# Four PSUM banks for the first eighth of the MLP's first product, and weight tiles of their own for the gates

## The chip, the cores and the metric

The kernel runs on one core of a Trainium2 chip. The metric is the time of one execution on the device in microseconds. Shown is the median of several runs; beside it stands one execution taken by the hardware profiler, from which all rows of this document come. Engines are named as in the profile: PE is the matmul engine (PEld its weight loads), DVE the vector engine, ACT the scalar engine, POOL the general one, SP the queue that issues the DMAs.

## What is computed

A decoder trunk of two layers over 256 tokens with 2048 channels in float32. The first layer mixes with a gated linear recurrence (RG-LRU), the second with dilated attention; a squared-ReLU MLP follows each.

```python
for i in range(DEPTH):                       # DEPTH = 2
    h = _rmsnorm(x, mix_norm[i])
    if i % N_MIXERS == 0:
        x = x + _rglru_block(h, ...)         # w_in, conv, gates w_a and w_x, scan, w_out
    else:
        x = x + _dilated_attention_block(h, ...)
    x = x + _mlp(_rmsnorm(x, mlp_norm[i]), mlp_w1[i], mlp_w2[i])
return _rmsnorm(x, final_norm)

def _mlp(h, w1, w2):
    u = jnp.square(jax.nn.relu(jnp.einsum('bsd,df->bsf', h, w1)))
    return jnp.einsum('bsf,fd->bsd', u, w2)  # 2048 -> 8192 -> 2048
```

In the recurrent block, the 2560 channels form ten heads of 256. Each head has two gates, two products with 256 x 256 matrices, that are fed by the head's convolved channels.

## The kernel before

**Units.** All weights come in units of 128 partitions x 2048 floats (1 MB). A unit is loaded into a `raw` tile (three of them, L82), and split into a high half `whi` (ACT, L102) and a low half `wlo` (DVE, L106). Each product is then the sum of three matmuls: high by high, high by low, low by high (`stand_w` L245 with the weights standing still and 256 tokens moving; `stand_x` L254 with the activations standing still). `whi` and `wlo` are rings of three tiles each: the split of a unit waits until the matmuls of the unit three back are done. The weights of the gates of one head are a unit too, but of half the width (1024 columns, `gate` L446), and take a whole place in the rings.

**Order.** Every engine's instructions stand in an order written out by hand. Items (L134) run one after another. Ahead of an item `before_unit` (L124) emits loads up to five units ahead, high halves up to two ahead and low halves up to two ahead; behind it `behind_unit` (L130) emits the next high half. What follows an item some items later (`after`, L161) is emitted behind it: the evacuation of its sums, the convolution, the gates' arithmetic. An engine that waits holds up all that is emitted behind. SP only issues loads; a load waits until the `raw` tile's low half was made.

**Recurrent block** (`plan_rec`, L431). From head 2 on a head's items are: P0 (first half of its recurrent channels), the gate of the head before, P1, P2 and P3 (second half, and the two halves of the multiplying branch). `xb_done` (L334) takes P0 and P1 into the convolution, `conv_split` (L354) splits the result for the gate, `gb_done` (L359) and `gelu_arg` (L366) take P2 and P3. `gate_run` (L373), `gate_sig`, `gate_exp`, `gate_mult`, `scan` and `y_split` (L387 to L429) follow the gate, one item apart. POOL does two products of a head, in `gate_exp` (L407, L408). The output projection follows in four chunks of 512 channels; `close_chunk` (L283) adds a chunk to the residual `xc` (`add_x`, L281), and the transposed chunk `xT` is the MLP's input. The factor of the norm, `rstdB`, is made last (`rstd_cols` L223, `rstd_rows` L235) and is not in `xT`: it is multiplied in when the sums of the first product are read (L486).

**PSUM.** Eight banks: four named `acc`, two `g`, two `tr`. Output projections, attention's products and most projections sum in `acc`; the gates and the MLP's first product in `g`; transposes in `tr`.

**MLP** (`plan_mlp`, L524). The first product's 8192 columns are done in eighths of eight units of 128 columns (j = 0 to 7), and the second product of an eighth runs between the units of the next. The first eighth has nothing to run between and so stands alone. `plan_start` (L534) runs its first two units, j = 0 and 4, in two pieces each, since the last chunk of `xT` comes late: 12 of 16 rows of j = 0, 12 of j = 4, then the last 4 of each. Then j = 1, 5, 2, 6, 3, 7 follow (L612). `u_done` (L481) reads the sums of a unit out of PSUM: DVE multiplies and clips (L486), ACT squares and makes the high half (L487, L489), DVE the low half a unit later (L495).

**Scopes.** Activations of a stage lie in a pool `lru` that is closed and opened again for each stage (L791 to L802), at the same place of the memory.

Of the kernel before, what the change touches and what calls it, by code (L numbers as in the profile page):

```python
# [10 lines left out]
F32 = mybir.dt.float32  # L11
F32R = mybir.dt.float32r
# [16 lines left out]
UW = 2048  # L29
# [12 lines left out]
HI_BUFS = 3  # L42
# [10 lines left out]
def trunk(ctx: ExitStack, tc: tile.TileContext, a: dict, out: bass.AP):  # L53
    nc = tc.nc
    P = 128

    perm = ctx.enter_context(tc.tile_pool(name="perm", bufs=1))
    wts = ctx.enter_context(tc.tile_pool(name="wts", bufs=1))
    psum = ctx.enter_context(tc.tile_pool(name="psum", bufs=1, space=bass.MemoryType.PSUM))
# [3 lines left out]
    units = []  # L63

    def unit(ap, width=UW):
        units.append({"ap": ap, "width": width})
        return len(units) - 1
# [6 lines left out]
    raw, split = {}, {}  # L74
# [14 lines left out]
    def make(i):  # L89
        if "load" in units[i]:  # L90
            units[i]["make"]()
            raw[i] = [(slice(0, UW), units[i]["source"]())]

    def new_hi(i):
        split[i] = (wts.tile([P, UW], F32R, name="whi", bufs=HI_BUFS),)

    def new_lo(i):
        split[i] += (wts.tile([P, UW], F32R, name="wlo", bufs=3),)

    def hi_piece(i, n):  # L100
        s, r = raw[i][n]
# [6 lines left out]
    def cut_hi(i):  # L108
        new_hi(i)
        for n in range(len(raw[i])):  # L110
            hi_piece(i, n)

    def cut_lo(i):
        new_lo(i)
        for n in range(len(raw[i])):
            lo_piece(i, n)
        del raw[i]
# [18 lines left out]
    def item(u, fn):  # L136
        items.append((u, fn))
# [21 lines left out]
    lru = Scope()  # L159

    def after(n, fn, *args):  # L161
        later.setdefault(now[0] + n, []).append((fn, args))
# [82 lines left out]
    def stand_w(ps, u, ks, w_at, first, last):  # L245
        hi, lo = split[u]
        for j, k in enumerate(ks):
            x = xT(k)
            s = slice((w_at + j) * 128, (w_at + j + 1) * 128)
            mm(ps, hi[:, s], x[:, 0:256], first and j == 0, False)  # L250
            mm(ps, hi[:, s], x[:, 256:512], False, False)
            mm(ps, lo[:, s], x[:, 0:256], False, last and j == len(ks) - 1)
# [12 lines left out]
    def acc_tile():  # L265
        return psum.tile([P, 512], F32, name="acc", bufs=4)

    accs = {}
# [255 lines left out]
    def plan_mlp(w1, w2, done):  # L524
        def plan_first(p, j):
            u = unit(w1[8 * p + j])

            def run():
                accs["u", p, j] = psum.tile([P, 512], F32, name="g", bufs=2)
                stand_w(accs["u", p, j][:, :S], u, range(KD), 0, True, True)  # L530
                after(0, u_done, p, j, accs.pop(("u", p, j)))
            item(u, run)

        def plan_start():  # L534
            us = [unit(w1[j]) for j in (0, 4)]
            for at, ks in enumerate((range(0, 12), range(12, 16))):
                for u, j in zip(us, (0, 4)):
                    def run(u=u, j=j, ks=ks, at=at):
                        if at == 0:
                            accs["u", 0, j] = psum.tile([P, 512], F32, name="g", bufs=2)  # L540
                        stand_w(accs["u", 0, j][:, :S], u, ks, ks[0], at == 0, at == 1)
                        if at == 1:
                            after(1 if j == 0 else 0, u_done, 0, j, accs.pop(("u", 0, j)))
                    item(u, run)
# [69 lines left out]
        for p in range(8):  # L614
# [5 lines left out]
            g = plan_group(p, 0) if p in GROUPS else {}  # L620
# [201 lines left out]
    for n in range(NCH):  # L822
        xg[n] = new_xg(n)
        rs = [wts.tile([P, UW], F32, name="raw", bufs=RAW_BUFS) for _ in range(3)] if n == 0 else rs
        for h in range(2 if n == 0 else 1):
            w = 2 if n == 0 else 4
# [11 lines left out]
        for h in range(2 if n == 0 else 1):  # L838
            w = 2 if n == 0 else 4
            for k in range(h * w, (h + 1) * w):  # L840
                nc.scalar.activation(t[:, k, 0:256], xg[n][:, k, :], AF.Identity, scale=pcol("mix0", 4 * n + k))
            for k in range(h * w, (h + 1) * w):
                nc.vector.scalar_tensor_tensor(t[:, k, 256:512], xg[n][:, k, :], pcol("mix0", 4 * n + k),  # L843
                                               t[:, k, 0:256].bitcast(F32), op0=OP.mult, op1=OP.subtract)
            for i in range(3):
                if n == 0 and h == 0:
                    new_hi(i)
                    new_lo(i)
                for at, (s, _) in enumerate(raw[i]):
                    if s.stop == n * 512 + (h + 1) * w * 128:  # L850
                        hi_piece(i, at)
                        lo_piece(i, at)
                        if s.start == 0:
                            accs["first", i] = acc_tile()
                            first[i] += (accs["first", i],)
                        ks = range(s.start // 128, s.stop // 128)
                        stand_w(accs["first", i][:, :S], i, ks, ks[0], s.start == 0, n == NCH - 1)
# [54 lines left out]
    for at in range(len(items) - 1, -1, -1):  # L912
        u = items[at][0]
# [86 lines left out]
```

## Time and profile before

| | us |
|---|---|
| median of three runs | 2189.44 (2188.41 to 2190.64) |
| the profiled execution's own time | 2186.37 |
| its span, first to last instruction | 2184.6 |
| PE busy in it | 2150.0 |
| DVE busy in it | 1602.2 |
| ACT busy in it | 1166.2 |

A row of the timeline reads: start and duration in us, engine, line, operation, the tile written and the tiles read, the shape, the count of merged instructions, and in brackets the idle time of the engine just before, with what ended it. A row of stretches reads: the stretch, its length, then for PE, PEld, DVE, ACT and POOL the busy time with the number of instructions in brackets, then the granted clock of PE, the share of the DMA engines and GB/s. A row of waits reads: engine, tile and line, what it waited for, us in total, times, the longest.

### The profile page before, as it was taken

To read this page: it belongs to the slowest core of one execution; us is meant where nothing else is said; L and a number is where in the kernel's file an instruction comes from. 1 tells how busy PE (TensorE), PEld (TensorE's weight loads), DVE (VectorE), ACT (ScalarE), POOL (GpSimd) and SP (SyncE) were. 2 spreads that over 40 slices of the span, in tenths; PEclk is the share of its full clock that TensorE was granted. 3 is DMA by queue.
4 is the path that set the end of the run, shared out by engine and by line. 5 is a ranking of instruction groups with operands and counts; after the bars stand their busy time and mean duration, and the time that the engine had idled before them with its cause. 6 is when DMAs were issued, how large, how long until landed. Compare 5 with 4: busy or idle time off the path is not lost.

```text
span 2184.6 us, 32102 instructions
## 1 busy us (share of the span) xinstructions
PE 2150.0 (98%) x13602; PEld 1944.2 (89%) x13602; DVE 1602.2 (73%) x1748; ACT 1166.2 (53%) x1261; POOL 81.3 (4%) x42
## 2 busy tenths in 40 slices
PE   7999999999999999999999999999999999999997
PEld 7999988999999999999888888889999999999996
DVE  8888865688888888787655555556888878887875
ACT  5777755554554555445545544555545544544543
POOL 2222100000000000000000000000000000000002
PEclk9999999999999999999999999999999999999999
DMA  6655565455465455554554444454564554545543
GB/s 220 213 190 190 183 222 180 174 203 221 138 248 189 177 195 207 185 223 163 179 198 156 172 174 173 157 191 161 206 231 144 222 213 154 218 187 193 212 175 134
DMA packets 61712, 413.56 MB, mean 189 GB/s; under 512 B 6784, under 2 KB 7168, under 8 KB 13440
## 3 DMA queue, kind: packets, MB, share of 16 engines
q1 hardware_dynamic: 61568, 411.51, 51.8%
q8 instruction: 106, 1.74, 0.3%
q14 instruction: 38, 0.31, 0.0%
HBM read 409.39 MB, written 2.10 MB: 188 GB/s over the span
## 4 chain that ended last, share of the span: by engine, by line
PE 80%; DVE 12%; ACT 5%; issue 2%; POOL 0%; DMA 0%; SPq 0%; DVEq 0%; ACTq 0%
PE acc L165 47%; PE g L165 27%; DVE wlo L106 7%; PE tr L165 4%; ACT whi L102 3%; DVE q L564 1%; ACT sT L181 1%; DVE xT L843 0%; DVE c L349 0%; DVE sT L182 0%; PE tr L205 0%; DVE aT L495 0%; DVE sw L506 0%; PE tr L664 0%; PE g L672 0%
## 5 line engine op out<-in xcount | busy, mean ns | idle before, releaser
L102 ACT ACTIVATE whi<-raw 128x2048 fp32r<-128x2048 f32 (+3 forms) x358 | 657.1, 1838 | 570.5 <-PE acc L165 313.9
L106 DVE TENSOR_TENSOR wlo<-raw,whi 128x2048 fp32r<-128x2048 f32 (+3 forms) x358 | 792.0, 2216 | 212.4 <-ACT whi L102 212.4
L165 PE MATMUL g<-xT,whi 128*128 128x256 f32 x4128 | 732.9, 281 | 5.8 <-DVE uu L486 5.8
L165 PEld LDWEIGHTS g<-xT,whi 128*128 128x128 f32 x4128 | 638.0, 188 | 15.2 <-DVE uu L486 6.3
L165 PE MATMUL g<-xT,wlo 128*128 128x256 f32 x2064 | 580.4, 281 | 2.1 <-DVE wlo L106 2.1
L165 PE MATMUL acc<-whi,aT 128*128 128x512 f32 x1840 | 580.5, 390 | 0.0
L165 PEld LDWEIGHTS acc<-whi,aT 128*128 128x128 f32 x1840 | 345.4, 188 | 69.6
L165 PEld LDWEIGHTS g<-xT,wlo 128*128 128x128 f32 x2064 | 395.3, 192 | 4.6 <-DVE wlo L106 4.6
L165 PE MATMUL acc<-wlo,aT 128*128 128x512 f32 x920 | 358.3, 389 | 0.0
L165 PE MATMUL acc<-whi,xT 128*128 128x512 f32 x768 | 245.9, 396 | 0.0
L165 PE MATMUL acc<-xT,whi 128*128 128x256 f32 x1248 | 223.5, 283 | 6.3 <-ACT whi L102 5.8
L165 PEld LDWEIGHTS acc<-wlo,aT 128*128 128x128 f32 x920 | 172.8, 188 | 33.5
L102 ACT ACTIVATE whi<-q 128x2048 fp32r<-128x2048 f32 x56 | 107.2, 1914 | 177.0 <-DVE q L564 137.8
L165 PEld LDWEIGHTS acc<-xT,whi 128*128 128x128 f32 x1248 | 195.0, 194 | 6.9 <-ACT whi L102 6.1
L165 PE MATMUL acc<-xT,wlo 128*128 128x256 f32 x624 | 178.2, 286 | 9.3 <-DVE wlo L106 9.0
L165 PEld LDWEIGHTS acc<-whi,xT 128*128 128x128 f32 x768 | 144.3, 188 | 30.7
L165 PE MATMUL acc<-wlo,xT 128*128 128x512 f32 x384 | 150.4, 392 | 0.0
L106 DVE TENSOR_TENSOR wlo<-q,whi 128x2048 fp32r<-128x2048 f32 x56 | 128.2, 2289 | 19.0 <-ACT whi L102 19.0
L165 PEld LDWEIGHTS acc<-xT,wlo 128*128 128x128 f32 x624 | 121.0, 194 | 12.0 <-DVE wlo L106 12.0
L102 ACT ACTIVATE whi<-qT 128x2048 fp32r<-128x2048 f32 x28 | 53.7, 1916 | 132.7 <-DVE qT L564 132.7
L106 DVE TENSOR_TENSOR wlo<-qT,whi 128x2048 fp32r<-128x2048 f32 x28 | 64.2, 2293 | 47.8 <-ACT whi L102 47.8
L165 PEld LDWEIGHTS acc<-wlo,xT 128*128 128x128 f32 x384 | 72.2, 188 | 15.1
(172 smaller groups left out, 1917.3 us busy)
## 6 DMA issues: line engine op xcount, KB each, us to landing
raw<-in_w SPq DMA_DIRECT2D x214, 1024.0 KB, 4.8
raw<-in_w_qkv SPq DMA_DIRECT2D x48, 1024.0 KB, 4.8
q<-in_w SPq DMA_DIRECT2D x42, 1024.0 KB, 6.9
raw<-in_w_in SPq DMA_DIRECT2D x35, 1024.0 KB, 4.8
raw<-in_w_out SPq DMA_DIRECT2D x20, 1024.0 KB, 4.8
raw<-in_w_o SPq DMA_DIRECT2D x16, 1024.0 KB, 4.8
raw<-in_w_g SPq DMA_DIRECT2D x10, 512.0 KB, 3.5
raw<-in_w_in SPq DMA_DIRECT2D x11, 256.0 KB, 6.1
```

The costliest lines, as they stand in the source:

```text
L102: nc.scalar.activation(split[i][0][:, s], r, AF.Copy)
L106: nc.vector.tensor_sub(split[i][1][:, s], r, split[i][0][:, s].bitcast(F32))
L165: nc.tensor.matmul(o, l, r, start=start, stop=stop, skip_group_check=True)
L181: nc.scalar.activation(hi_out, src, AF.Copy)
L564: nc.vector.tensor_add(q[to], q[a], q[b])
```

## The change

First, the sums of the first eighth (p = 0) of each MLP's first product are put in `acc` banks, of which there are four, and not in `g`, of which there are two; the other seven eighths stay in `g`. Second, a unit that is narrower than 2048 columns, which only the gates' ten units are, is split into tiles `ghi` and `glo` of its own (two of each, 1024 columns, in the stage's pool) and not into the rings `whi` and `wlo`. No instruction is added, removed or moved in any engine's order.

```diff
+    def cut_tile(i, name, bufs):
+        width = units[i].get("width", UW)
+        if width < UW:
+            return lru.tile([P, width], F32R, name="g" + name, bufs=2)
+        return wts.tile([P, UW], F32R, name="w" + name, bufs=bufs)
+
     def new_hi(i):
-        split[i] = (wts.tile([P, UW], F32R, name="whi", bufs=HI_BUFS),)
+        split[i] = (cut_tile(i, "hi", HI_BUFS),)
 
     def new_lo(i):
-        split[i] += (wts.tile([P, UW], F32R, name="wlo", bufs=3),)
+        split[i] += (cut_tile(i, "lo", 3),)
...
             def run():
-                accs["u", p, j] = psum.tile([P, 512], F32, name="g", bufs=2)
+                accs["u", p, j] = acc_tile() if p == 0 else psum.tile([P, 512], F32, name="g", bufs=2)
                 stand_w(accs["u", p, j][:, :S], u, range(KD), 0, True, True)
...
                         if at == 0:
-                            accs["u", 0, j] = psum.tile([P, 512], F32, name="g", bufs=2)
+                            accs["u", 0, j] = acc_tile()
                         stand_w(accs["u", 0, j][:, :S], u, ks, ks[0], at == 0, at == 1)
```

`acc_tile` (L265) is `psum.tile([P, 512], F32, name="acc", bufs=4)`.

## The prediction

> **What bounds the kernel now.** I read the page's totals first, then what the matmul engine waited for, over the span and inside two stretches.
>
> ```profile
> span 2184.6 us, 32102 instructions
> PE 2150.0 (98%) x13602; PEld 1944.2 (89%) x13602; DVE 1602.2 (73%) x1748; ACT 1166.2 (53%) x1261; POOL 81.3 (4%) x42
> ```
>
> PE is busy for 2150.0 of 2184.6 us. No instruction is added or removed by the change, so the most that it can win is idle PE time and what follows from it.
>
> ```profile
> PE acc L165 <- DVE wlo L106: 9.0, 9, 3.1
> PE g L165 <- DVE uu L486: 5.8, 2, 2.9
> PE acc L165 <- ACT whi L102: 5.8, 2, 5.4
> PEld g L165 <- DVE uu L486: 6.3, 2, 3.2
> PE acc L165 <- DVE wlo L106: 1.8, 6, 0.3
> PE acc L165 <- DVE wlo L106: 2.4, 1, 2.4
> ```
>
> Columns: total us, times, longest. The first four rows are of the whole span, the fifth is of 100 to 260 us (the gates' loop), the sixth of 60 to 100 us. Two things can be won by this diff: the two waits on `uu` (one at the start of each MLP) and the six small ones in the gates' loop. The rest of the `acc` rows lies before 60 us, where no gate has run yet, and the wait of 2.4 us has another cause (below).
>
> **Part one: four banks for the first eighth.** At the start of the first MLP:
>
> ```profile
> 388.45 1.39 DVE L281 TENSOR_TENSOR xc<-xc,acc 128x512 f32<-128x512 f32 x2 [0.66 <-PE acc L165]
> 391.11 2.29 DVE L106 TENSOR_TENSOR wlo<-raw,whi 128x2048 fp32r<-128x2048 f32 x1 [1.27 <-ACT whi L102]
> 399.66 3.71 ACT L102 ACTIVATE whi<-raw 128x2048 fp32r<-128x2048 f32 x2 [1.30 <-PE g L165]
> 400.99 0.38 PE L238 MATMUL tr<-con,rs 128*128 128x128 f32 x2
> 401.61 2.29 DVE L106 TENSOR_TENSOR wlo<-raw,whi 128x2048 fp32r<-128x2048 f32 x1 [2.27 <-ACT whi L102]
> 403.28 0.36 ACT L241 ACTIVATE rstdB<-tr 128x256 f32<-128x256 f32 x1
> 403.81 0.75 DVE L486 SCALAR_TENSOR_TENSOR uu<-g,rstdB 128x256 f32<-128x256 f32 x2
> 404.29 0.50 PE L165 MATMUL g<-xT,whi 128*128 128x256 f32 x2 [2.91 <-DVE uu L486]
> 404.48 2.28 DVE L106 TENSOR_TENSOR wlo<-raw,whi 128x2048 fp32r<-128x2048 f32 x1
> 404.60:408.00 3.40, 3.40 (x32) 3.40 (x31) 2.83 (x3) 1.22 (x4) 0.00 (x0) 1.00 0.86 306
> ```
>
> Blocks j=0 and j=4 hold both `g` banks. They are emptied by L486, which needs `rstdB` (L241), which stands on ACT behind two weight splits. The third block, j=1, waits for a `g` bank until the first L486 ends. With `acc` it takes one of four banks. The blocks j=0 and j=4 take the banks of the output projection's third chunk and j=1 and j=5 those of its last; the last chunk's `acc` was read at 388.45 + 1.39 = 389.84. The fifth block, j=2, is the first that comes back to a bank of j=0. It starts two blocks later, and a block is 48 matmuls, 5.1 us at the 32 in 3.40 us of the last row (a stretch: PE's count stands in the first bracket, the granted clock third from the end), so the L486 at 403.81 is about 7 us early for it.
>
> What is late next? For j=1 the low half was done at 391.11 + 2.29 = 393.40. For j=5 it is done at 401.61 + 2.29 = 403.90, wanted at about 401.2 + 5.1 = 406.3; for j=2 at 406.76, wanted at 411.4. Later splits wait for the block that frees their tile and move with PE. So nothing catches the gain, and I price it by the weight loads' wait, 6.3 us for both MLPs (the matmul row, 5.8, counts only from the modelled end of the last transpose). The second MLP has the same picture:
>
> ```profile
> 1488.30 0.38 PE L238 MATMUL tr<-con,rs 128*128 128x128 f32 x2
> 1491.60 0.50 PE L165 MATMUL g<-xT,whi 128*128 128x256 f32 x2 [2.92 <-DVE uu L486]
> 1492.10:1495.50 3.40, 3.40 (x18) 3.40 (x18) 2.64 (x3) 1.06 (x3) 0.00 (x0) 0.52 0.93 316
> 85.80:89.20 3.40, 3.40 (x18) 3.40 (x18) 3.33 (x4) 3.38 (x6) 3.10 (x2) 0.52 0.95 317
> ```
>
> The last two rows are again stretches of 3.4 us behind a stall. Behind the one at 404 (row above) PE did 32 matmuls at clock 1.00; behind the one at 1491 it did 18 at 0.52, and as few behind the 2.4 us stall before 84.5. A stall can thus cost 14/32 of 3.4 us, 1.5 us, on top. In the profiled execution one of the two `uu` stalls paid it, so 1.5 us goes with them. Bounds: 0 (neither pays) and 3.0 (both). Part one: 6.3 + 1.5 = 7.8 us.
>
> The Trainium skill (TensorE: Matmul & The Clock Gate, Part 1) says that the clock is halved after at least one idle window of about 3.4 us, in windows that run freely. By that rule a stall of 3.2 us would be too short, nothing would be saved beyond the 6.3, and the time is that of the rival on the clock below. The row at 1492 disagrees, 0.52 after a shorter stall.
>
> **Part two: the gates' own weight tiles.** Gate units leave the ring of three `whi` and three `wlo`. One head of the steady loop (a projection P0, the gate, then P1, P2, P3):
>
> ```profile
> 122.16 1.92 ACT L102 ACTIVATE whi<-raw 128x2048 fp32r<-128x2048 f32 x1 [0.77 <-PE acc L165]
> 127.60 1.92 ACT L102 ACTIVATE whi<-raw 128x2048 fp32r<-128x2048 f32 x1 [3.52 <-PE acc L165]
> 130.56 1.90 ACT L102 ACTIVATE whi<-raw 128x2048 fp32r<-128x2048 f32 x1
> 121.42 0.69 DVE L182 TENSOR_TENSOR chl<-c,chl 128x512 fp32r<-128x512 f32 x1 [1.22 <-ACT chl L181]
> 125.59 0.69 DVE L423 TENSOR_TENSOR i<-i,gb 128x512 f32<-128x512 f32 x1
> 122.36 1.22 DVE L106 TENSOR_TENSOR wlo<-raw,whi 128x1024 fp32r<-128x1024 f32 x1
> 126.54 2.28 DVE L106 TENSOR_TENSOR wlo<-raw,whi 128x2048 fp32r<-128x2048 f32 x1
> 129.85 0.76 DVE L182 TENSOR_TENSOR aT<-i,aT 128x256 fp32r<-128x256 f32 x2 [1.04 <-ACT aT L181]
> 134.11 5.58 DVE L106 TENSOR_TENSOR wlo<-raw,whi 128x2048 fp32r<-128x2048 f32 x2
> 135.77 0.39 PE L165 MATMUL acc<-xT,whi 128*128 128x256 f32 x2
> 136.45 0.39 PE L165 MATMUL acc<-xT,wlo 128*128 128x256 f32 x1 [0.29 <-DVE wlo L106]
> 136.68 0.40 PE L165 MATMUL acc<-xT,whi 128*128 128x256 f32 x2
> 119.63 9.54 SPq L87 DMA_DIRECT2D raw<-in_w_in  x3
> raw<-in_w_in SPq DMA_DIRECT2D x35, 1024.0 KB, 4.8
> ```
>
> The split at 127.60 is the high half of P2. Its ring slot is that of the unit three back, P0, whose matmuls end at 127.5; so ACT stands 3.52 us, the aT split behind it is late, DVE stands 1.04 us at 129.85, and P2's low half (134.11, ends 136.40) is late for PE at 136.0. With the gate out of the ring the unit three back is the P3 of the head before, which had freed its slot at 122.16 (first row). The split then waits for its data: loaded from 119.63, 4.8 us later at 124.4, ended at 126.4. The aT split follows, since L423 is done at 125.59 + 0.69 = 126.28, and DVE goes on at 126.54 + 2.28 = 128.82, 1.03 us earlier. P2's low half ends at 135.4, 0.6 us early.
>
> What PE lost: from the row at 135.77 the next should start 0.23 later (two matmuls), it starts 0.68 later, and the pair behind 0.23 instead of 0.12 later: 0.57 us a head, six heads, 3.4 us. Is DVE the next bound?
>
> ```profile
> 127.51:152.68 25.17, 24.88 (x219) 24.68 (x217) 22.38 (x29) 19.09 (x23) 5.43 (x2) 1.00 0.55 190
> 135.42 2.13 POOL L407 TENSOR_TENSOR c<-c,i 128x512 f32<-128x512 f32 x1 [19.73 <-ACT i L394]
> 68.20 1.30 POOL L408 TENSOR_TENSOR gb<-gb,gw 128x512 f32<-128x512 f32 x1
> 63.29 0.63 ACT L181 ACTIVATE chl<-c 128x512 fp32r<-128x512 f32 x1 [4.76 <-POOL c L347]
> ```
>
> A head lasts 25.17 us. PE needs 25.17 - 0.57 = 24.60; DVE, without the 1.04, 24.13, with its other wait of 1.22 kept. So PE decides, by 0.47. The unknown is POOL. The two splits at 134.11 took 5.58 us, 1.0 more than twice 2.29, while POOL ran L407: they get in each other's way, and today the second split, which is early, pays. ACT's chain to L407 moves by about 2.1 us (the split at 130.56 can start when its data are there: the raw tile comes free with the gate's low half at 122.36 + 1.22 = 123.58, the load lands 4.8 us later at 128.4), so L407 comes near 133.3, and P2's low half starts near 133.1. If POOL comes first, it delays that split by at most its own 1.30, to about 136.7, later than today's 136.4. Bounds: 3.4 us won to 6 x 0.3 = 2 lost. I take 3.4, since DVE comes first and gains up to 0.47 more on PE with each head.
>
> The 2.4 us stall before 84.5 stays: ACT is without a pause from 63.29, where it waited for POOL's convolution, and no split of a tile waits there. The tiles' 16 KB per partition cost no instruction; the next scope lays its tiles over the same space, but opens only behind the output projection, when the last gate is long done. So 0.
>
> **Sum.** 7.8 + 3.4 = 11.2 us. The profiled execution took 2186.37, so 2175.2 for a like one; the median of the runs is 2189.44, 3.07 above it, and gives 2178.2.
>
> **Rivals.**
> - The gates' half gives nothing, because P2's low half now meets POOL or DVE's chain doesn't get ahead. For it: the 0.2 us between 133.1 and 133.3, and DVE's load. Against it: 0.6 us of room at P2. Time: 2189.44 - 7.8 = 2181.6.
> - The clock isn't part of it: whether a stall meets a half-clock stretch is chance (one of two did), and if the timed runs paid none, 6.3 + 3.4 gives 2179.7. By the rule of the Trainium skill told above, this is the case that holds.
> - Part one doesn't do what it says: j=1 finds another wait as long. For it: the wait's name is inferred. Against it: PE starts at 404.29, between the ends of the two L486 (a pair of 0.75 from 403.81), as it would if the first one held it, and its weights and the other bank are there by 394. Time: 2189.44 - 3.4 = 2186.0, not to be told from no change.
> - Slower: both POOL products (L407, L408) come ahead of P2's low half in every head. At 1.30 each it ends at 135.4 + 2.6 = 138.0, PE stalls 2.0 us for 0.45 now, and about half of such stalls also pay 1.5 us of clock, as before 85.8. Six heads: 6 x 1.55 + 3 x 1.5 = 13.8 us lost, less part one's 7.8: 2189.44 + 6.0 = 2195.4. It decides from the point where L408 starts before the split; against it, L408 waits for ACT L397, behind L407's own inputs. The Trainium skill (SBUF — State Buffer, on the shared port pair of VectorE and GpSimd) has this as an exclusive lock, first come first served; the 5.58 us agree with such a lock.
>
> **Chances.** Forecast 0.60 (own range 2175.5 to 2180.5), clock 0.10, gates nothing 0.18, part one nothing 0.07, slower 0.05. The range 2175.0 to 2184.0 holds the first three, the gates' case with part of its possible loss, and about 1 us of scatter (the runs spread from 2188.41 to 2190.64). About 0.2%, 4.4 us, is what a measurement of this kernel can tell from no change; the first three cases lie beyond it: faster 0.87, within 0.08, slower 0.05.
>
> **What would show it.** Right: no wait of PE on `uu`; the matmuls of j=1 directly behind the two transposes of L238, at 401.2 or a little earlier; clock 1.00 through the start of both MLPs; the 3.52 us of ACT before P2's split gone; no PE wait on `wlo` between 100 and 260 us; heads of 24.6 us; the 2.4 us stall still there. Wrong: a wait of PE on `acc` behind add_x or L486, heads of 25.2 us or more, or a POOL product ahead of P2's low half.

## The result

| | before, us | after, us | ratio, 95% interval |
|---|---|---|---|
| first comparison (4 and 4 runs) | 2188.93 (2187.90 to 2190.64) | 2173.74 (2173.12 to 2174.57) | 0.993 (0.9913 to 0.9947) |
| second comparison (21 and 5 runs) | 2186.27 (2180.39 to 2190.34) | 2175.25 (2173.29 to 2175.83) | 0.995 (0.9937 to 0.9963) |
| the profiled execution's own time | 2186.37 | 2173.91 | |

The change wins 15.2 us in the first comparison and 11.0 us in the second. The forecast was 11.2 us won and 2178.2 us, in a range of 2175.0 to 2184.0; the median of the first comparison lies 1.3 us below that range, that of the second 0.25 us inside it. The two waits that the prediction named went, at about their price. What was sized wrong is the clock that goes with one of them.

The page's totals of the changed kernel, and then what PE waited for (total us, times, longest). Lines of the code stand six further down than before: L165 is L171, L238 is L244, L486 is L492, L407 is L413.

```profile
span 2172.1 us, 32089 instructions
PE 2144.1 (99%) x13602; PEld 1940.1 (89%) x13602; DVE 1600.6 (74%) x1748; ACT 1167.5 (54%) x1261; POOL 78.9 (4%) x42
```

PE's waits, the first three rows over the span, the fourth between 60 and 100 us:

```profile
PE acc L171 <- DVE wlo L112: 8.1, 4, 2.7
PE acc L171 <- ACT whi L108: 6.1, 2, 5.9
PE g L171 <- DVE wlo L112: 2.2, 12, 0.2
PE acc L171 <- DVE wlo L112: 2.6, 1, 2.6
```

No wait on `uu` is left. Between 100 and 260 us PE waits for nothing any more. Between 60 and 100 us the stall of 2.4 us before the loop is still there, now 2.6 us.

The timeline at the start of the first MLP:

```profile
395.73 0.38 PE L244 MATMUL tr<-con,rs 128*128 128x128 f32 x2
395.87 0.48 PE L171 MATMUL acc<-xT,whi 128*128 128x256 f32 x2
394.40 3.72 ACT L108 ACTIVATE whi<-raw 128x2048 fp32r<-128x2048 f32 x2 [1.30 <-PE acc L171]
398.02 0.36 ACT L247 ACTIVATE rstdB<-tr 128x256 f32<-128x256 f32 x1
398.56 0.75 DVE L492 SCALAR_TENSOR_TENSOR uu<-acc,rstdB 128x256 f32<-128x256 f32 x2
```

And stretches of 3.4 us at the start of both (the count of matmuls in the first bracket, the granted clock third from the end):

```profile
395.87:399.27 3.40, 3.40 (x32) 3.40 (x31) 2.92 (x4) 2.78 (x4) 0.00 (x0) 1.00 0.00 0
1480.92:1484.32 3.40, 3.40 (x33) 3.40 (x31) 2.92 (x4) 2.78 (x4) 0.00 (x0) 1.00 0.00 0
```

The chain behind the transposes is unchanged: two splits on ACT, then `rstdB`, then L492. But j = 1 no longer stands behind it. It starts 0.14 us after the transposes instead of 3.30 us, and L492 reads j = 0 while j = 1 runs. The clock is 1.00 at both starts.

One head of the gates' loop (the gate starts at 125.99):

```profile
117.89 1.91 ACT L108 ACTIVATE whi<-raw 128x2048 fp32r<-128x2048 f32 x1
120.72 1.92 ACT L108 ACTIVATE whi<-raw 128x2048 fp32r<-128x2048 f32 x1 [0.92 <-PE acc L171]
126.07 1.92 ACT L108 ACTIVATE whi<-raw 128x2048 fp32r<-128x2048 f32 x1 [1.91 <-PE acc L171]
125.33 0.76 DVE L188 TENSOR_TENSOR aT<-i,aT 128x256 fp32r<-128x256 f32 x2
129.43 5.59 DVE L112 TENSOR_TENSOR wlo<-raw,whi 128x2048 fp32r<-128x2048 f32 x2
130.95 1.91 POOL L413 TENSOR_TENSOR c<-c,i 128x512 f32<-128x512 f32 x1 [18.59 <-ACT i L400]
132.82 3.35 POOL L414 TENSOR_TENSOR gb<-gb,gw 128x512 f32<-128x512 f32 x1
115.92 9.85 SPq L87 DMA_DIRECT2D raw<-in_w_in  x3
```

The same head as one stretch:

```profile
125.99:150.62 24.63, 24.63 (x218) 24.63 (x217) 22.21 (x29) 19.30 (x23) 5.22 (x2) 1.00 0.57 193
```

The high halves of P1, P2 and P3 are the first three rows. P2's starts 5.3 us ahead of the gate; before, it started 0.1 us behind it, after the wait of 3.52 us. The wait of 1.91 us that ACT now has is P3's, and nobody is late by it. DVE no longer waits at `aT`. P2's low half (the first of the two at 129.43) starts 3.4 us behind the gate instead of 6.6 us, 1.5 us ahead of POOL's L413. PE is busy through the whole head, 24.63 us.

**Where the 12.5 us between the two profiled spans are.** The same stages of both kernels: up to the second head's gate, seven heads of gates, up to the transposes of L238, the start of the first MLP, up to the second start, that start, the rest. Of before:

```profile
0.00:102.34 102.34, 88.60 (x678) 86.67 (x679) 83.64 (x128) 64.59 (x92) 28.84 (x21) 0.95 0.63 215
102.34:279.13 176.79, 174.95 (x1491) 172.61 (x1490) 155.90 (x197) 133.58 (x161) 38.04 (x14) 1.00 0.56 194
279.13:400.99 121.86, 121.80 (x609) 102.88 (x608) 66.44 (x56) 67.62 (x82) 3.23 (x2) 1.00 0.54 191
400.99:404.29 3.30, 0.39 (x5) 0.14 (x3) 2.69 (x3) 2.68 (x4) 0.00 (x0) 1.00 0.00 0
404.29:1488.30 1084.01, 1082.89 (x6397) 959.05 (x6397) 750.42 (x822) 553.46 (x604) 0.00 (x0) 1.00 0.51 187
1488.30:1491.60 3.30, 0.38 (x5) 0.14 (x3) 2.69 (x3) 2.67 (x4) 0.00 (x0) 1.00 0.00 0
1491.60:2184.60 693.00, 680.99 (x4428) 622.73 (x4428) 540.39 (x543) 341.57 (x318) 11.23 (x5) 0.99 0.51 190
```

And of after:

```profile
0.00:101.35 101.35, 86.51 (x679) 84.41 (x680) 84.40 (x129) 67.71 (x96) 28.87 (x21) 0.98 0.63 217
101.35:273.81 172.46, 172.46 (x1491) 171.50 (x1489) 155.97 (x200) 134.57 (x161) 35.86 (x14) 1.00 0.58 199
273.81:395.73 121.92, 121.86 (x609) 102.94 (x608) 64.38 (x54) 64.82 (x78) 2.87 (x2) 1.00 0.54 190
395.73:395.87 0.14, 0.14 (x4) 0.14 (x3) 0.00 (x0) 0.14 (x1) 0.00 (x0) 1.00 0.00 0
395.87:1480.78 1084.91, 1083.76 (x6399) 959.98 (x6398) 752.86 (x824) 556.04 (x607) 0.00 (x0) 1.00 0.51 186
1480.78:1480.92 0.14, 0.14 (x5) 0.14 (x3) 0.00 (x0) 0.14 (x1) 0.00 (x0) 1.00 0.00 0
1480.92:2172.10 691.18, 679.19 (x4431) 620.95 (x4428) 543.02 (x545) 344.12 (x321) 11.25 (x5) 1.00 0.51 191
```

| stage | difference, us | what it is |
|---|---|---|
| start-up | -0.99 | clock 0.95 against 0.98, untouched code |
| heads with gates | -4.33 | part two |
| up to the transposes | +0.06 | |
| first MLP's start | -3.16 | part one, the wait |
| first MLP and attention | +0.90 | the same work, a little slower |
| second MLP's start | -3.16 | part one, the wait |
| the rest | -1.82 | mostly the half-clock stretch behind the stall at 1491 |
| sum | -12.50 | |

So from profile to profile the forecast was 1.3 us off (2175.2 for 2173.91), and without the two stages in which the clock differs (-0.99 and -1.82) the change won 9.7 us, as 6.3 + 3.4 had it. That it agrees to the tenth is luck: the gates gave 0.9 us more than their 3.4, and 0.90 us was given back behind the first MLP's start. The medians differ by 2.7 us more than the profiles: before's profiled execution lies 2.6 us below its median, after's 0.2 us above. The experiments ask whether part one, part two or the clock is worth more in a usual run than in the profiled one.

### The profile page after: what moved, and what is told of

Read it like the earlier page. It is cut to its first block, busy times and chain, and to the rows that moved or that the text cites. A ratio compares the mean times of both kernels' runs of the same rounds, so it can differ in the third digit from the quotient of the medians.

```text
span 2172.1 us, 32089 instructions
## 1 busy us (share of the span) xinstructions
PE 2144.1 (99%) x13602; PEld 1940.1 (89%) x13602; DVE 1600.6 (74%) x1748; ACT 1167.5 (54%) x1261; POOL 78.9 (4%) x42
## 3 DMA queue, kind: packets, MB, share of 16 engines
q8 instruction: 106, 1.74, 0.3%
## 4 chain that ended last, share of the span: by engine, by line
PE 83%; DVE 10%; ACT 4%; issue 1%; POOL 0%; DMA 0%; SPq 0%; DVEq 0%; ACTq 0%
PE acc L171 53%; PE g L171 24%; DVE wlo L112 6%; PE tr L171 4%; ACT whi L108 2%; DVE q L570 1%; ACT sT L187 1%; DVE sT L188 0%; PE tr L211 0%; DVE aT L501 0%; DVE sw L512 0%; PE tr L670 0%; PE g L678 0%; DVE xT L849 0%; DVE sw L514 0%
## 5 line engine op out<-in xcount | busy, mean ns | idle before, releaser
L108 ACT ACTIVATE whi<-raw 128x2048 fp32r<-128x2048 f32 (+2 forms) x348 | 646.8, 1860 | 562.2 <-PE acc L171 336.5
L112 DVE TENSOR_TENSOR wlo<-raw,whi 128x2048 fp32r<-128x2048 f32 (+2 forms) x348 | 779.9, 2245 | 214.9 <-ACT whi L108 214.7
L171 PE MATMUL g<-xT,whi 128*128 128x256 f32 x3616 | 642.4, 281 | 0.0
L171 PE MATMUL acc<-whi,aT 128*128 128x512 f32 x1840 | 580.5, 390 | 0.0
L171 PEld LDWEIGHTS g<-xT,whi 128*128 128x128 f32 x3616 | 559.1, 188 | 8.7
L171 PE MATMUL g<-xT,wlo 128*128 128x256 f32 x1808 | 508.5, 281 | 2.2 <-DVE wlo L112 2.2
L171 PEld LDWEIGHTS acc<-whi,aT 128*128 128x128 f32 x1840 | 345.4, 188 | 69.6
L171 PE MATMUL acc<-wlo,aT 128*128 128x512 f32 x920 | 358.3, 389 | 0.0
L171 PEld LDWEIGHTS g<-xT,wlo 128*128 128x128 f32 x1808 | 346.2, 191 | 4.6 <-DVE wlo L112 4.6
L171 PE MATMUL acc<-xT,whi 128*128 128x256 f32 x1760 | 309.7, 281 | 6.5 <-ACT whi L108 6.1
L171 PEld LDWEIGHTS acc<-xT,whi 128*128 128x128 f32 x1760 | 270.7, 191 | 7.5 <-ACT whi L108 6.3
L171 PE MATMUL acc<-xT,wlo 128*128 128x256 f32 x880 | 247.2, 281 | 8.3 <-DVE wlo L112 8.1
L171 PE MATMUL acc<-whi,xT 128*128 128x512 f32 x768 | 245.9, 396 | 0.0
L171 PEld LDWEIGHTS acc<-wlo,aT 128*128 128x128 f32 x920 | 172.8, 188 | 33.4
L171 PEld LDWEIGHTS acc<-xT,wlo 128*128 128x128 f32 x880 | 168.0, 191 | 9.6 <-DVE wlo L112 9.4
L171 PEld LDWEIGHTS acc<-whi,xT 128*128 128x128 f32 x768 | 144.3, 188 | 30.6
L171 PE MATMUL acc<-wlo,xT 128*128 128x512 f32 x384 | 150.4, 392 | 0.0
L171 PEld LDWEIGHTS acc<-wlo,xT 128*128 128x128 f32 x384 | 72.2, 188 | 15.1
```

The source lines that it names most:

```text
L108: nc.scalar.activation(split[i][0][:, s], r, AF.Copy)
L112: nc.vector.tensor_sub(split[i][1][:, s], r, split[i][0][:, s].bitcast(F32))
L171: nc.tensor.matmul(o, l, r, start=start, stop=stop, skip_group_check=True)
```

## The experiments

The first four kernels of the table were timed beside the kernel before on one chip, the last four on another; two repeats at the end ran once each on a third. Times in the text are medians, those of the table means, and a difference is to the kernel before on the same chip (2188.91 on the first, 2186.27 on the second, 21 runs each). Each run also lists its mean granted clock to three places. From it I worked out what the run lost, (1 - clock) times its span, and what is left of its time then. One step in the last place is 2.2 us of a run, so only means over runs, and differences between kernels, say something. The column counts every half-clock stretch: also those of start-up, which five profiles show twice, one once and six not at all, and 2.8 to 4.5 us a run behind the last matmul, where they cost PE nothing.

| kernel, runs | mean us | lost to the clock | rest |
|---|---|---|---|
| before, first chip, 21 | 2188.9 | 10.5 | 2178.3 |
| banks alone, 5 | 2180.3 | 6.5 | 2173.8 |
| gates alone, 11 | 2183.0 | 10.5 | 2172.5 |
| before with the stalls filled, 11 | 2185.7 | 6.6 | 2179.1 |
| a third transpose, 5 | 2174.6 | 6.1 | 2168.5 |
| before, second chip, 21 | 2186.0 | 9.2 | 2176.8 |
| gates' high halves alone, 10 | 2181.7 | 9.4 | 2172.3 |
| gates' low halves alone, 10 | 2186.8 | 9.2 | 2177.6 |
| after with its stalls filled, 5 | 2171.9 | 2.2 | 2169.7 |
| after, 5 | 2174.9 | 7.0 | 2167.9 |

### Each part alone

The first kernel has only the two `acc_tile()` edits, the second only `cut_tile` and its two calls.

> The kernel before with the first half of the change alone: the first eighth of the first MLP product sums in the four acc banks, the gates' weights stay in the shared rings. Theory A (the prediction's terms): 6.3 us of wait and 1.5 us of clock go, 7.8 us below the kernel before, so about 2181.2. Theory B (the unprofiled runs of the kernel before lose more half-clock stretches behind the two stalls than the one that its profile shows): 10 to 12 us below, about 2178, and less scatter between runs. Theory C (the surplus of the change over its forecast lies in the gates' half): 7 to 8 us below here and 7 us or more in the run with the gates alone.

> The kernel before with the second half alone: the gates' units in tiles of their own, the first eighth still in the two g banks. Theory A: 3.4 us below the kernel before, about 2185.6, no wait of PE on wlo between 100 and 260 us, both waits of about 2.9 us on uu still there. Theory B: the same 3.4 to 4 us here. Theory C: 7 us or more below, about 2182.

The banks alone took 2181.01 us, 7.9 us won, ratio 0.9964 (0.9951 to 0.9976). The forecast for part one, 7.8 us, is met, but not by its terms. The wait is gone, 6.3 us. The table gives 4.0 us to the clock instead of 1.5, and the rest fell by only 4.5 us. In its profile the heads' loop, which this kernel doesn't change, ran at a slower pace of the matmuls, 1.8 us over seven heads (178.55 us against 176.79, see the last experiment), so the agreement in the total is partly chance. The 10 to 12 us of Theory B didn't come, nor did less scatter (standard deviation 1.6 us, before 1.7).

The gates alone took 2183.08 us, 5.8 us won, ratio 0.9975 (0.9966 to 0.9984). The clock has no part in it (10.5 us in both), as it should be with both `uu` stalls still there. The interval, 3.5 to 7.4 us, begins just above the forecast of 3.4 us and holds the 4.33 us of the stage table. Both parts work: 7.9 + 5.8 = 13.7 us, between the 15.2 and the 11.0 of the whole change's two comparisons. On the same chip as the parts the whole was timed only with a third transpose (below), at 13.9 us.

The profile of the gates alone shows more of the clock than the kernel before did. What PE waited for on `uu`:

```profile
PE g L171 <- DVE uu L492: 5.8, 2, 2.9
```

Its first matmuls behind the first of the two stalls:

```profile
400.26 0.80 PE L171 MATMUL g<-xT,whi 128*128 128x256 f32 x2 [2.92 <-DVE uu L492]
```

Stretches behind the first stall, and one behind the second:

```profile
400.26:403.66 3.40, 3.40 (x16) 3.40 (x17) 3.15 (x4) 1.54 (x4) 0.00 (x0) 0.50 0.86 287
403.66:407.06 3.40, 3.40 (x20) 3.40 (x20) 0.00 (x0) 0.00 (x0) 0.00 (x0) 0.60 0.88 330
407.06:410.46 3.40, 3.40 (x31) 3.40 (x31) 1.41 (x5) 1.61 (x1) 0.00 (x0) 1.00 0.00 0
1491.44:1494.84 3.40, 3.40 (x17) 3.40 (x18) 3.15 (x4) 1.55 (x4) 0.00 (x0) 0.56 0.81 275
```

Here both stalls of 2.92 us were followed by the half clock, and the first one for twice as long: 16 and 20 matmuls where 31 fit. In the trace's record of the granted clock the stretches are 3.41 us long or twice that, and each 3.41 us lose half, 1.7 us. The five profiles that have both stalls unfilled (before, before again, gates alone, high halves alone, low halves alone) have 1, 2, 3, 2 and 3 stretches behind them. That is a mean of 2.2, or 3.7 us, where the prediction counted one.

Which stalls bring the half clock can be read from these traces. In each trace all changes of the clock stand whole multiples of 3.413 us apart, so the span can be laid out in windows of that length whose borders the changes share. A stall of 2.92 us lies in one window or is divided by a border. The eight stalls that were followed by the half clock left PE idle for 1.99 to 2.92 us of one window, and the half clock began at that window's end. The two that were not were divided: 1.74 and 1.17 us (before, first stall), 1.06 and 1.86 us (high halves alone, second stall). The stall of 2.3 to 2.6 us ahead of the loop fits as well: ten of its eleven unfilled copies put 1.99 to 2.61 us into one window and brought the half clock, and the one that was divided (before again, 1.11 and 1.15 us) didn't. The limit thus lies between 1.86 and 1.99 us of idle time in a window here. In start-up it is less sharp (five windows near 15 us with 1.5 to 1.8 us were followed by the half clock, others as idle were not), and the second stretch of a double one isn't explained by it. No run moved a stall against the windows on purpose.

### Which half of the gates' tiles

One kernel keeps only the high halves in tiles of their own, the other only the low halves; both without the banks:

```diff
     def new_lo(i):                       # high halves alone
-        split[i] += (cut_tile(i, "lo", 3),)
+        split[i] += (wts.tile([P, UW], F32R, name="wlo", bufs=3),)
...
     def new_hi(i):                       # low halves alone
-        split[i] = (cut_tile(i, "hi", HI_BUFS),)
+        split[i] = (wts.tile([P, UW], F32R, name="whi", bufs=HI_BUFS),)
```

> The gates' half with the high tiles alone: the gates' high halves in tiles of their own, their low halves still in the shared ring of three, the first eighth in the g banks. Theory A (the slot of whi is what ACT stood for, 3.52 us a head): all of the gates' gain, as with both tiles, 3.4 to 5.8 us below the kernel before, no wait of PE on wlo between 100 and 260 us. Rival (the low ring matters as well): less than half of it, the small waits partly there.

> The gates' half with the low tiles alone. Theory A: no difference from the kernel before, six waits of 0.3 us on wlo between 100 and 260 us, ACT's 3.52 us there. Rival: 1 us or more below.

High halves alone: 2181.82 us, 4.4 us won, ratio 0.998 (0.9971 to 0.9989), and PE waits for nothing between 100 and 260 us. Low halves alone: 2186.35 us, no difference, ratio 1.0003 (0.9993 to 1.0013). In that kernel's profile PE's wait between 100 and 260 us stands nearly as before (1.8 us, six times):

```profile
PE acc L171 <- DVE wlo L112: 1.5, 6, 0.3
```

And ACT's wait before P2's high half is the one of before:

```profile
126.03 1.92 ACT L108 ACTIVATE whi<-raw 128x2048 fp32r<-128x2048 f32 x1 [3.52 <-PE acc L171]
```

So part two works through the ring of high halves alone, on the path that the prediction gave: P2's high half waits for P0's slot. The tiles `glo` are worth nothing measurable by themselves. The 4.4 us, with equal clock losses (9.4 and 9.2), agree with the 4.33 us of the stage table.

### What the clock costs behind a stall

The kernel before, with the two stalls filled by transposes that nobody reads. It does all the work of the kernel before and 24 transposes more at each MLP's start:

```diff
         state["rstdB"] = rb
+        if scope[0] in ("mlp", "end"):
+            fill = psum.tile([P, 2, S], F32, name="tr", bufs=2)
+            for _ in range(24):
+                nc.tensor.transpose(fill[:, 0, 0:128], ident, ident)
```

> The kernel before, with nothing of the change, but with 24 transposes of the unit matrix into a tr bank that is free, behind the norm's two transposes at the start of each MLP: 24 x 0.109 = 2.6 us of work of PE that nobody reads, in the 3.1 us in which it stalls on uu. The wait for the banks stays, PE is not idle in it. Theory A: only the clock of one stall in two is saved, 1.5 us below the kernel before at most, since the next block starts when it did. Theory B: the clock of both stalls in nearly every run, 3 to 5 us below. If idle time behind PE costs no clock: no difference.

It took 2185.73 us, 3.2 us won, ratio 0.9985 (0.9976 to 0.9994), though j = 1 starts as late as before. The timeline at the first start:

```profile
402.20 0.38 PE L238 MATMUL tr<-con,rs 128*128 128x128 f32 x2
402.42 2.78 PE L246 MATMUL tr<-con 128*128 128x128 f32 x24
405.50 0.51 PE L165 MATMUL g<-xT,whi 128*128 128x256 f32 x2 [0.29 <-DVE uu L490]
```

A stretch behind each start:

```profile
405.50:408.90 3.40, 3.40 (x29) 3.40 (x30) 3.15 (x4) 1.55 (x4) 0.00 (x0) 1.00 0.71 270
1492.48:1495.88 3.40, 3.40 (x29) 3.40 (x30) 3.15 (x4) 1.55 (x4) 0.00 (x0) 1.00 0.75 275
```

The distance from L238's transposes to j = 1 is 3.30 us, as without the filling, and the clock behind it is 1.00 both times. So this is the clock's share by itself: 3.2 us by the medians (1.3 to 5.3 by the interval), 4.0 us by the listed clocks, against 1.5 us in the sum. The interval alone would not rule out the 1.5.

If stalls cost clock wherever they are, the changed kernel has more to win: some lie in start-up, and one before the loop. The next kernel is the kernel after, with matmuls of a zero tile in front of the first product's chunks 2 to 4 and of P2 of head 2. Their sums are read by nobody, and all else is unchanged (the zero tile, which DVE clears once at the start, is left out here):

```diff
+    def fill(n):
+        t = psum.tile([P, 2, S], F32, name="tr", bufs=2)
+        for _ in range(n):
+            nc.tensor.matmul(t[:, 0, :], zero[:, 0:128], zero, start=True, stop=True)
...
+                if (h, j, g) == (2, 0, 1):
+                    fill(20)
                 ps = acc_tile() if u > len(first) else psum.tile([P, 512], F32, name="g", bufs=2)
...
+                        if i == 0 and n:
+                            fill((0, 10, 10, 18)[n])
                         stand_w(accs["first", i][:, :S], i, ks, ks[0], s.start == 0, n == NCH - 1)
```

> The changed kernel with work that nobody reads in the stalls that it still has: 10, 10 and 18 matmuls of 256 zero columns ahead of the second, third and fourth chunk of the first products (stalls of 1.4, 1.4 and 2.7 us near 16, 22 and 28 us) and 20 ahead of the unit that stalls 2.6 us near 80 us. No wait is shorter. If stalls cost clock behind them as the filled stall of the kernel before says (3.2 us for two stalls of 3.1 us), it is 1 to 3 us faster than the changed kernel, its mean clock nearer to 0.998 or 0.999. If not: the same time, or some tenths more where the filling is longer than the stall.

> The changed kernel, once more, beside the filled one on the same chip and with the kernel before in the same rounds. Theory B: about 15 us below the kernel before; the mean clock of its runs about 0.9975 against 0.995 of the kernel before, that is some 5 us of half clock fewer, and some 10 us without the clock. A second profile of the same program also shows whether the pace of the 256-column matmuls behind the first MLP's start (0.1178 us) belongs to the program or to the execution.

The filled kernel took 2172.04 us (2171.39 to 2172.39), ratio to the kernel before 0.9936 (0.9924 to 0.9949); the kernel after, beside it, 2175.25 us. That is 3.2 us less for 58 matmuls more, a little above the 1 to 3 expected, and it is the fastest kernel here. The listed clock is 0.999 in all five of its runs, and its trace has no half clock between 14 us, where the record begins, and the last matmul. The kernel after missed its own expectation: it is 11.0 us below the kernel before and not about 15, with 2.2 us fewer of half clock and not some 5, and 8.9 us without the clock. PE's waits on `acc` that remain in its profile:

```profile
PE acc L171 <- ACT whi L108: 6.3, 1, 6.3
PE acc L171 <- DVE wlo L112: 4.6, 5, 1.4
```

The stretch behind the filled stall before the loop:

```profile
83.48:86.88 3.40, 3.40 (x29) 3.40 (x30) 3.36 (x5) 2.69 (x6) 1.77 (x1) 1.00 0.64 202
```

The same stretch in the kernel after:

```profile
84.00:87.40 3.40, 3.40 (x18) 3.40 (x18) 3.33 (x4) 3.40 (x6) 2.78 (x2) 0.53 1.02 342
```

29 matmuls instead of 18 in 3.4 us. The wait of 6.3 us lies ahead of the first matmul; the others, of up to 1.4 us, left the clock at 0.999. The five times lie within 1.0 us (standard deviation 0.4 us), those of the kernel after, on the same chip, within 2.5 us (1.1 us) and those of the kernel before within 10 us (2.3 us; 21 runs, the others 5). That points to the half-clock stretches as a large part of the scatter. The pace of the next section is another.

### The 0.9 us given back, and the scatter of one program

Behind the first MLP's start the kernel after is 0.90 us slower than before for the same work at clock 1.00. To see whether the exact moment at which j = 1 starts decides this, a third transpose was put behind the two of L244 in the kernel after, with nothing else changed:

```diff
                                 state["rstd"][:, t:t + 1].to_broadcast([P, P]), ident)
+        if scope[0] in ("mlp", "end"):
+            nc.tensor.transpose(tr[:, 1, 0:128], state["rstd"][:, 0:1].to_broadcast([P, P]), ident)
```

> The changed kernel with one more transpose of 128 columns (0.11 us, read by nobody) behind the norm's two at the start of each MLP. In the changed kernel's profile the 256-column matmuls behind these transposes start every 0.1178 us in the first MLP and every 0.1133 us in the second, over some 288 matmuls, 1.3 us. If the pace is set by the exact moment at which the first of them follows the transposes, one more transpose can flip it in either MLP: 1.1 us faster to 1.5 us slower. If it is set by the place in the program (addresses, banks), both paces stay and the time is 0.2 us more.

It took 2175.01 us, 13.9 us less than before, ratio 0.9937 (0.9925 to 0.995). The matmuls behind the first start kept the slower pace, so a shift by one transpose doesn't decide it. Then two programs were profiled once more:

> The kernel before, profiled once more. Its first profile has 1063 quick (under 0.1155 us from start to start) and 223 slow 256-column matmuls in the recurrent loop, the quick pace behind both MLPs' starts, and one half-clock stretch behind the two uu stalls; its own time, 2186.4, lay below the median of 21 runs, 2188.9. If the pace belongs to the program, the counts are the same within some tens and only the clock stretches differ. If it belongs to the execution, the counts differ by hundreds, at 0.0044 us each: 500 are 2.2 us.

> The banks' half alone, profiled once more. Its first profile has 525 quick and 746 slow matmuls in the recurrent loop, which its change does not touch. Same question: the same counts again, or other ones.

The kernel before took 2186.67 us (2188.00 in another run of that round), and the banks alone 2178.58 us (2181.01 as median before), one time each. The kernel before's stretch behind the first `uu` stall, which was at clock 1.00 in its first profile, is now

```profile
403.46:406.86 3.40, 3.40 (x19) 3.40 (x20) 3.14 (x4) 1.54 (x4) 0.00 (x0) 0.64 0.74 258
```

so the same stall of the same program does and doesn't bring the half clock, by where it falls in the windows (2.47 us in one here, 1.74 and 1.17 us there). What differs between the two profiles of the banks is the loop of gates, which this kernel doesn't touch: 874 slow starts of a matmul between 90 and 262 us in the first, 503 in the second (starts are recorded in whole ns; slow is 116 to 119 ns after the one ahead, quick up to 115; the expectations count only those within the projections). In the kernel before there are 316 and 408. The heads show it in us: with the shared ring of high halves most take 25.2 us, and those in which most matmuls are slow 25.8. Of seven heads the banks have four and two long ones (178.55 and 177.32 us for the seven), the kernel before one and one. The pace in the loop is thus part of the scatter too. The second profiles come from another chip, so that may be the chip or the execution.

Behind the MLPs' starts the pace goes with the program. In all six profiles with the first eighth in `acc` banks, the second one of the kernel after among them, 287 of the first 288 distances are slow behind the first start and at least 284 quick behind the second. With `g` banks the first start is quick in four profiles and slow in two (gates alone, low halves alone). So the 0.90 us is no scatter of one profile but a price of this program; the prediction has no term for it. Why a stretch takes the one or the other stays open.

## Why the prediction was right, and where it failed

**The wait on `uu`, 6.3 us: right.** The distance from the transposes to j = 1 fell from 3.30 to 0.14 us at both starts, 6.32 us. Nothing else caught j = 1, j = 5 or j = 2: PE has no wait between 260 and 410 us.

**The clock, 1.5 us with bounds 0 and 3.0: this step failed.** In its place the runs show 3.2 us (stalls filled, by the medians) to 4.0 us (stalls filled and banks alone, by the listed clocks), and 3.7 us by the stretches of five profiles. For the change itself the listed clocks give 2.2 us in the second comparison (9.2 against 7.0); in the first, after's four runs lost 5.4 us, which is 5.1 less than the 10.5 of the 21 runs of before on the first chip (whether the first comparison ran on that chip isn't known). Two things were wrong in the step. One profile was read as the usual run: it had one stretch behind the two stalls, the mean of five profiles is 2.2. Its one stall in two without the half clock was luck: if a stall of 2.92 us begins anywhere in a window of 3.41 us, and about 1.9 us in one window are needed, a border divides it into shorter parts in some 0.9 of 3.4 cases, one in four (an estimate from the figures above). And the upper bound gave each stall at most one stretch, where the gates-alone profile has one stall that paid two (0.50, then 0.60): the bound from such rows is 4 stretches, 6.8 us, not 3.0. With 4.0 for this term the sum is 6.3 + 4.0 + 3.4 = 13.7 us and the time 2189.44 - 13.7 = 2175.7. That is still inside the range, so this term by itself doesn't give the 15.2 us of the first comparison. With 5.0 us for the gates (below) and the 0.9 us given back the sum is 14.4 us, between the measured 15.2 and 11.0. The rest of the change, without the clock, adds up nearly as forecast: 9.7 us in the sum and between the profiles, 8.9 us in the second comparison (2176.8 against 2167.9).

**The rule on the clock.** The prediction gave 0.10 to the case that the clock isn't part of it, by the rule of the Trainium skill (TensorE: Matmul & The Clock Gate, Part 1) that the half clock follows at least one idle window of about 3.4 us. The filled stalls show that case wrong: of the ten stalls of 2.9 us in the five profiles, eight were followed by the half clock, and where they were filled or gone it didn't come. Here 1.99 us of idle time in one window was enough; none of these stalls filled a whole one. The stretches' length, 3.41 us, is the window that the page gives.

**The gates, 3.4 us: right, a little small.** Heads take 24.63 us (24.60 forecast, 25.17 before), so six give 3.2 us; the seventh, which the prediction left out, gives 0.5 us (25.17 to 24.65), and the other 0.6 us of the 4.33 is one head of before at the slow pace (25.77 us). With tiles of their own for the gates no head of any profile is that long. Over the six profiles in which the high halves share their ring seven heads take 176.7 to 178.6 us, 177.45 on average, against 172.49 with both tiles (five profiles, within 0.2 us): 5.0 us rather than 3.4. High halves alone show the forecast's path by itself, 4.4 us. That PE decides and not DVE is borne out: PE is busy for all of the 24.63 us, DVE for 22.21.

**A step inside it that was wrong without harm.** The prediction had P2's split wait for its data until 124.4, and so come 3.2 us earlier, with P2's low half 1.0 us earlier. The split starts as soon as its slot is free (120.72, `<-PE acc`), 5.4 us earlier against the gate, and the low half 3.2 us earlier. Its load is earlier too: the three loads of the head begin 10.1 us ahead of the gate (115.92) where they began 7.9 us ahead (119.63 against 127.51). The load waits for DVE's split that frees the raw tile (a low half ends at 115.89 in the kernel after), so an earlier DVE moved the transfers that feed it, which the prediction had taken as fixed. That settled its one unknown: POOL's L413 comes 1.5 us behind P2's low half, not 0.2 us, and the split that collides is again the second of the pair, which is early (5.59 us for the two, 5.58 before).

**The slower rival** didn't happen, and so its price of 1.30 us for each POOL product wasn't tested. That figure is from a row at 68.20 ahead of the loop; L414 takes 3.35 us in six heads of the loop, where it runs beside DVE's splits, and 1.29 to 1.35 us in the others. How much of that is waiting, and how much a split behind it would lose, no run here shows; the two splits beside POOL lost 1.0 us together. The longer product agrees with the lock of which the Trainium skill tells (SBUF — State Buffer, on the port pair that VectorE and GpSimd share).

**The other rivals** fall by the parts run alone: 5.8 us for the gates, 7.9 us for the banks. The stall before 84.5 stayed (2.4, then 2.6 us), and the tiles' space cost nothing: 121.86 and 121.92 us from the last gate to the transposes.

**What stays open.** The gates alone win 5.8 us in the times, 4.33 in the stage table and 5.0 over all profiles; where the last 0.8 us comes from isn't known. What sets the pace isn't either. The two comparisons differ by 4 us in what the change wins; the clocks of the first one's runs of the kernel before are not listed, so the clock's share in that isn't known. Nor was it found why the kernel before lost 10.5 us to the clock on one chip and 9.2 on the other, or why its profiled execution, with a usual clock of 0.995, lies 2.6 us below its median.

## What to carry to other kernels

A stall of the matmul engine of some 3 us costs its own length and, on average here, 1.6 to 2.0 us more in clock behind it. Price both, and the second from several executions or their listed clocks, since behind one stall a profile shows anything from nothing to two stretches. Where a stall can't be removed, matmuls that nobody reads can hold the clock (3.2 us won by 58 of them here). When units of different use share a ring of tiles, count the slots: the odd one pushes another unit's split behind matmuls that end late, and three steps on that is a stall of PE (here ACT's 3.52 us, DVE's 1.04 us, then 0.57 us of PE a head).

## What the runs showed of the hardware

The clock falls to half for 3.41 or 6.83 us behind stalls of 1.4 to 3.1 us, in some executions of a program and not in others. Behind the 21 stalls of 2.3 to 2.9 us past start-up it did so in the 18 that left PE idle for 1.99 us or more of one window of 3.413 us, and not in the three that left at most 1.86 us. With such stalls filled, five runs lay within 1.0 us.

PE also has two paces at the same granted clock. In the kernel after, on both sides of the transposes in the output projection, the timeline's first and last row of each run of groups (a group is three matmuls of 256 columns):

```profile
384.05 0.39 PE L171 MATMUL acc<-xT,whi 128*128 128x256 f32 x2
387.44 0.39 PE L171 MATMUL acc<-xT,whi 128*128 128x256 f32 x2
389.02 0.40 PE L171 MATMUL acc<-xT,whi 128*128 128x256 f32 x2
395.38 0.40 PE L171 MATMUL acc<-xT,whi 128*128 128x256 f32 x2
```

The two runs as stretches:

```profile
384.05:387.44 3.39, 3.39 (x32) 3.39 (x31) 2.12 (x2) 1.77 (x1) 0.00 (x0) 1.00 0.71 278
389.02:395.38 6.36, 6.36 (x56) 6.36 (x55) 2.44 (x9) 4.59 (x11) 0.00 (x0) 1.00 0.48 167
```

Ten groups take 3.39 us, 0.1130 us for a matmul; behind the transposes eighteen take 6.36 us, 0.1178 us. The clock is 1.00 in both, and PE waits for nothing. For a thousand matmuls that is 4.8 us, which no count of instructions and no wait shows.
